# A two-block transformer kernel on one core: first products on the raw stream, 64-row matmuls in pairs, and the class-ordered copy on ScalarE

## The chip, the cores and the metric

The kernel runs on one core of a Trainium2 chip. The metric is the device time of one execution in microseconds (us); lower is better. Several executions of a kernel are timed and the median stands for it.

## What is computed

The reference runs two blocks of two layers each on a stream `x` of 512 tokens by 1024 features. Only the first block is touched. Its layer 0 mixes with gated linear attention (`gla`) and differential attention, its layer 1 with dilated attention over three patterns; each is followed by a feed-forward layer.

```python
def rmsnorm(x, g):
    y = xf * lax.rsqrt(jnp.mean(xf * xf, axis=-1, keepdims=True) + EPS)
    return (y * g.astype(jnp.float32)).astype(x.dtype)
def even_mixer(h, ...):                  # h = rmsnorm(x, norm_mix[0])
    z = h @ w_in                         # aq, ak, av, ag, ar, bq, bk, bv
    log_a = log_sigmoid(ar @ w_a2 + b_a) / GLA_TAU
    oa = rmsnorm(gla(aq, ak, av, log_a), gla_gain) * silu(ag)
    ob = diff_attention(rmsnorm(bq), rmsnorm(bk), bv, lam)   # (softmax(q1 k1^T) - lam softmax(q2 k2^T)) v
    return concat([oa, rmsnorm(ob, diff_gain) * ...]) @ w_out
def odd_mixer(h, ...):                   # q, k normed per head; dilations 1, 4, 16
    ...                                  # dilations 4 and 16 read the tokens by residue class
```

## The kernel before, in words

**Layout.** The stream is kept transposed: eight tiles `x` of 128 features by 512 tokens, in halves of 256 tokens. All large products are float32 made of three fp32r matmuls (`mm3`, line 392): each operand is split into a rounded part and a rest, and hi·hi, hi·lo, lo·hi are added up in one PSUM bank (`gm` by features, `gt` by tokens).

**Weights.** One load of 512 KB (`raw`, four buffers, `wdma`, line 329) holds four 128-row blocks of 256 columns. Two units are cut from it: ScalarE (ACT) copies the rounded part `whi`, VectorE (DVE) subtracts the rest `wlo` (`split`, line 257). A unit serves 12 matmuls of 256 columns in the first passes.

**The norm.** `square` and `norm` (lines 456 and 497) square the stream on ACT into `nsq`, add on DVE, sum over features by a matmul with ones (`nst`), take 1/rms by a chain of 12 small DVE operations (`rsqrt_small`, line 442), spread it by a matmul (`nbc`) to `nrb`, and then make `nt` = x times the norm's weight times `nrb` (DVE), `hh` (ACT) and `hl` (DVE) for each of the eight tiles. In `run` (line 1684) this stands ahead of the first product of the program.

**The first products.** `firsts` (line 707) computes three 256-column weight blocks (k twice, q once) for tokens 0 to 255 and then for tokens 256 to 511: 2 x 144 matmuls of 256 columns, in six banks.

**What sets the order.** The program is written out by a planner in Python: `Clock` (line 98) holds an estimated time of each engine, `tick` (line 771) runs after each tile's matmuls and lets due tasks (`spawn`) and chores (weight splits, rests of intermediate products) issue their next step; `finish` (line 792) steps tasks until given ones are done. Each engine then runs its own instructions in the order written, and waits by semaphores. All instructions carry line 172, that of the wrapper, so this text goes by tile names.

**Even mixer** (line 889). `k_norm` and `q_scale` (lines 944, 989) norm k and prepare q: `qst` (matmul) gives sums of squares of q, a DVE chain on `qv` makes the scale `cc`. `diff_unit` (line 1034) is one head and one block of 128 queries: for each of the two softmaxes a matmul `ds` of 64 rows (float32, two passes) by 128 to 512 columns, then a mask product (`bf_mc`, `bf_ident`), then the softmax. The two softmaxes lie in rows 0 to 63 and 64 to 127 of `q` and `bk`. `gla` (line 1089) makes masked scores `att` and states; `gla_out` (line 1173) is one head: for each of four token tiles one 128-row product `oa<-att,av` and one or two 64-row products `oa<-qd,state`, evacuated to `oraw`, and then `o_norm` (line 974), whose result is split into `mh`, `ml`.

**Odd mixer** (line 1190). The products of the second and third pattern read `ph`, `pl`: `hh`, `hl` with the tokens ordered by class (t mod 4). GpSimd (POOL) makes them by 16 copies of 128x512, issued after the first pattern's q and k. At that time k's norms run on DVE, then the q chains, and PE goes on to the scores `os` and the value products `gt`.

## Time and profile before

| quantity | value |
|---|---|
| median of 3 executions | 3385.5 us (3381.23 to 3389.09) |
| the profiled execution | 3386.47 us |
| its span | 3384.7 us (1.8 us lie around it) |
| busy: PE, weight load, DVE, ACT, POOL | 98%, 86%, 62%, 37%, 1% |
| chain that ended last | PE 89%, DVE 6%, ACT 3%, DMA 1%, issue 1% |

In a timeline row stand the start, the length, the engine, the operation with the tiles it writes and reads, rows\*columns of the array that it uses, the shape that streams, the number of instructions put together, and in brackets the idle time before it with what ended that. A float32 matmul shows as two instructions (two passes). The matmuls overlap at their ends, so a pace is read from starts, not from lengths. In a windows row the clock granted to PE stands as a fraction of its full level.

### The profile page before, as it was taken

The numbers are of one execution on the slowest core, as the hardware profiler recorded it, in microseconds if no ns is written. First come the engines' busy times: TensorE is split into PE (matmuls) and PEld (weight loads), VectorE is DVE, ScalarE is ACT, GpSimd is POOL, SyncE is SP. The second block draws the span as 40 slices with busy tenths as digits, with TensorE's granted clock in tenths as the row PEclk, the third lists the DMA queues.
The fourth block names the chain that finished last, engine by engine and source line by source line (L and its number), as shares of the span: only waits on it lengthen the run. The fifth ranks groups of instructions, "written<-read, shape, count | busy, mean of one in ns | idle before, by whom it ended". The sixth has DMA issues, their size and how long they took to land.

```text
span 3384.7 us, 48370 instructions
## 1 busy us (share of the span) xinstructions
PE 3327.9 (98%) x19172; PEld 2898.5 (86%) x19172; DVE 2113.2 (62%) x4570; ACT 1251.6 (37%) x2526; POOL 28.0 (1%) x29
## 2 busy tenths in 40 slices
PE   7999999989999999999999989999999999999999
PEld 7688888888898888988888987988898889998888
DVE  5757988775669778764455867855663335463333
ACT  5554434334454334322112356422333223443231
POOL 0000000020000000000000000000000000000000
PEclk9999999999999999999999999999999999999999
DMA  3122444412224444443333311344532233222332
GB/s 112 63 63 80 128 141 131 131 63 74 70 88 125 132 136 131 129 146 111 125 119 119 94 42 44 122 153 144 163 100 85 95 100 100 94 89 93 100 99 70
DMA packets 105845, 355.73 MB, mean 105 GB/s; under 512 B 12673, under 2 KB 18962, under 8 KB 105618
## 3 DMA queue, kind: packets, MB, share of 16 engines
q1 hardware_dynamic: 105618, 352.64, 33.2%
q8 instruction: 150, 2.46, 0.3%
q14 instruction: 77, 0.63, 0.1%
HBM read 350.50 MB, written 2.10 MB: 104 GB/s over the span
## 4 chain that ended last, share of the span: by engine, by line
PE 89%; DVE 6%; ACT 3%; issue 1%; DMA 1%; SPq 0%; DVEq 0%; ACTq 0%
PE gm L172 81%; PE gt L172 4%; ACT ap L172 1%; PE ds L172 1%; DVE wlo L172 1%; PE ss L172 1%; DVE nt L172 1%; PE oa L172 1%; DVE amx L172 0%; DVE rs_t L172 0%; PE os L172 0%; ACT L172 0%; DVE ksq L172 0%; DVE x L172 0%; PE opo L172 0%
## 5 line engine op out<-in xcount | busy, mean ns | idle before, releaser
L172 PE MATMUL gm<-hh,whi 128*128 128x512 f32 (+1 forms) x2872 | 1041.0, 362 | 4.9 <-ACT hh L172 4.1
L172 PE MATMUL gm<-hl,whi 128*128 128x512 f32 (+1 forms) x2872 | 1034.5, 360 | 1.2 <-DVE hl L172 1.2
L172 PE MATMUL gm<-hh,wlo 128*128 128x512 f32 (+1 forms) x2872 | 1031.9, 359 | 3.5 <-DVE wlo L172 3.4
L172 DVE TENSOR_TENSOR wlo<-raw,whi 128x512 fp32r<-128x512 f32 (+1 forms) x1028 | 661.7, 681 | 91.9 <-ACT whi L172 91.5
L172 ACT ACTIVATE whi<-raw 128x512 fp32r<-128x512 f32 (+1 forms) x1028 | 581.4, 617 | 291.6 <-PE gm L172 104.8
L172 PEld LDWEIGHTS gm<-hh,wlo 128*128 128x128 f32 x2872 | 543.9, 189 | 87.1 <-DVE wlo L172 4.2
L172 PEld LDWEIGHTS gm<-hh,whi 128*128 128x128 f32 x2872 | 544.7, 190 | 73.5 <-ACT hh L172 4.4
L172 PEld LDWEIGHTS gm<-hl,whi 128*128 128x128 f32 x2872 | 544.7, 190 | 68.4 <-DVE hl L172 1.8
L172 PE MATMUL gm<-mh,whi 128*128 128x512 f32 (+1 forms) x1696 | 577.5, 341 | 0.0
L172 PE MATMUL gm<-ml,whi 128*128 128x512 f32 (+1 forms) x1696 | 573.5, 338 | 1.2 <-DVE ml L172 1.2
L172 PE MATMUL gm<-mh,wlo 128*128 128x512 f32 (+1 forms) x1696 | 572.1, 337 | 0.0
L172 DVE TENSOR_TENSOR ga<-ga,gm 128x512 f32<-128x512 f32 (+1 forms) x110 | 68.1, 633 | 497.5 <-PE gm L172 328.4
L172 PEld LDWEIGHTS gm<-mh,wlo 128*128 128x128 f32 x1696 | 322.2, 190 | 34.8
L172 PEld LDWEIGHTS gm<-ml,whi 128*128 128x128 f32 x1696 | 322.5, 190 | 29.4 <-DVE ml L172 1.6
L172 PEld LDWEIGHTS gm<-mh,whi 128*128 128x128 f32 x1696 | 322.4, 190 | 29.1 <-issue 0.9
L172 ACT ACTIVATE ga<-gm 128x512 f32<-128x512 f32 (+1 forms) x110 | 58.8, 554 | 715.9 <-PE gm L172 715.9
L172 DVE SCALAR_TENSOR_TENSOR macc<-rawm,sc,macc 128x256 f32<-128x256 f32 x504 | 244.0, 484 | 15.4
L172 DVE SCALAR_TENSOR_TENSOR x<-gm,modt,x 128x256 f32<-128x256 f32 (+1 forms) x184 | 106.0, 608 | 226.3 <-PE gm L172 226.2
L172 PEld LDWEIGHTS gm<-hc,whi 128*128 128x128 f32 x736 | 136.0, 190 | 29.0 <-ACT whi L172 1.6
L172 DVE SCALAR_TENSOR_TENSOR cy<-gm,vec,cy 128x511 f32<-128x511 f32 (+1 forms) x176 | 127.8, 747 | 47.9 <-ACT cy L172 44.7
L172 PE MATMUL gm<-hc,whi 128*128 128x256 f32 x736 | 146.2, 282 | 1.4 <-ACT whi L172 1.4
L172 ACT ACTIVATE nsq<-x 128x256 f32<-128x256 f32 x160 | 60.8, 416 | 179.4 <-DVE x L172 175.9
(300 smaller groups left out, 3530.7 us busy)
## 6 DMA issues: line engine op xcount, KB each, us to landing
raw<-in_ffn_w_dram SPq DMA_DIRECT2D x256, 512.0 KB, 4.3
rawm<-in_w_mod_dram SPq DMA_DIRECT2D x144, 512.0 KB, 4.4
raw<-in_ffn_w_up_dram SPq DMA_DIRECT2D x88, 512.0 KB, 3.7
raw<-in_ffn_w_down_dram SPq DMA_DIRECT2D x40, 512.0 KB, 3.7
raw<-in_od_w_in_dram SPq DMA_DIRECT2D x36, 512.0 KB, 3.8
raw<-in_ev_w_in_dram SPq DMA_DIRECT2D x24, 512.0 KB, 3.9
raw<-in_w_in_c_dram SPq DMA_DIRECT2D x16, 512.0 KB, 4.1
raw<-in_w_in_a_dram SPq DMA_DIRECT2D x10, 512.0 KB, 4.5
```

What stands on the lines that cost most here:

```text
L172: return f(*args, **kwargs)
```

## The change

It has three parts.

1. **The start.** The stream is loaded in five transfers instead of sixteen, all loads of the start are put in another order, and the norm's weights (`vec`, 16 columns), the first weight load and a part of the constants are issued on ScalarE's queue. `begin` makes `hh`, `hl` from x times the norm's weight as x lands, with no 1/rms in it; `stats` computes 1/rms (`rs` by token on partitions, `rb` spread over partitions) as a task beside the products. 1/rms is then applied where products are evacuated: `scaled` on DVE for `bk`, `qd`, `kr`, `sg`, `ar`, ACT's `scale` for `bv`, `av`, and three more small DVE operations in each of the four `q_scale` chains. `constants` (POOL) runs after `stats`.
2. **Pairs.** `diff_unit` issues the two 64-row `ds` products back to back in two banks and then the two mask products. `gla_out` handles two heads at once, its 64-row products alternating between rows 0 to 63 and 64 to 127; the four `o_norm` tasks depend on it.
3. **The copy.** The 16 class-ordered copies go from POOL to ACT, as a task `turn` that issues one each 0.9 us of the planner's time.

```diff
-        self.x = []
-        for k in range(NK):
-            t = self.xp.tile([P, S], F32, name=f"x{k}")
-            nc.sync.dma_start(t[:, HALF[0]], a["xT"][k][:, HALF[0]])
-            self.x.append(t)
...
+        nc.scalar.dma_start(self.vec[:, :16], a["vec"][:, :16])
+        load(0, 2, 0)
+        if plan is not None:
+            self.wdma(nc.scalar)
+        load(2, 5, 0)
+        load(5, 8, 0)
+        if plan is not None:
+            self.wdma()
+        load(0, 4, 1)
+        nc.scalar.dma_start(self.cst[:, :256], a["cst"][:, :256])
+        load(4, 8, 1)
         if plan is not None:
             for _ in range(2):
                 self.wdma()
...
+    def begin(self):
...
+        def one(p, k):
+            (hi, lo), x, G = [t[:, HALF[p]] for t in self.hx[k]], self.x[k][:, HALF[p]], self.v("norm_mix", k)
+            nc.scalar.activation(hi, x, AF.Copy, scale=G)
+            nc.vector.scalar_tensor_tensor(lo, x, G, hi.bitcast(F32), op0=OP.mult, op1=OP.subtract)
...
+        for k in range(NK):
+            one(0, k)
+            if k < 4 and k % 2 == 0 and self.plan is not None:
+                self.wsplit()
+                self.flush()
+        self.chore(later())
+        self.stat = self.spawn(self.stats(), front=True, banks=1)
+
+    def stats(self):
...
+                for i in range(2):
+                    nc.scalar.activation(sq[:, i * 256:(i + 1) * 256], self.x[k + i][:, HALF[p]], AF.Square)
+                sums.append(sq)
+                if k:
+                    yield later()
+                    nc.vector.tensor_add(sums[0], sums[0], sq)
...
+    def scaled(self, ps, name, scale=1.0):
+
+        t = self.g(name)
+        self.nc.vector.scalar_tensor_tensor(t, ps, scale, self.rb, op0=OP.mult, op1=OP.mult)
+        return t
...
-        pre = self.firsts([w(8), w(9), w(6)])
+        pre = self.firsts([w(8), w(9), w(6)], [(h, HALF[0], HALF[0], None), (h, HALF[1], HALF[1], self.flush)])
+        self.finish([self.stat])
+        self.constants()
...
+            if rows is not None:
+                by = lambda x: x.rearrange("p (t j) -> p t j", j=nh)
+                rw = rows[:, :, None].to_broadcast([P, 4, nh])
+                nc.vector.tensor_mul(by(v), by(p), rw)
+                nc.vector.tensor_mul(by(v), by(v), rw)
+                p = v
...
-        for j in range(2):
-            s = self.ps("ds", w)
+
+        ss = [self.ps("ds", w) for _ in range(2)]
+        for j, s in enumerate(ss):
             r = slice(j * 64, j * 64 + 64)
             self.mm(s, q[r, n * P:(n + 1) * P], k[r, :w], stop=False)
+        for s in ss:
             self.mm(s[:, n * P:], self.mbf["ident"], self.mbf["mc"], start=False)
...
         for t in range(4):
-            p = self.ps("oa", P)
-            self.mm(p, av[t][:, hd * P:(hd + 1) * P], att[t][:, hd * P:(hd + 1) * P], stop=False)
+            ps = [self.ps("oa", P) for _ in range(2)]
+            for j, p in enumerate(ps):
+                hd = 2 * c + j
+                self.mm(p, av[t][:, hd * P:(hd + 1) * P], att[t][:, hd * P:(hd + 1) * P], stop=False)
             ns = [n for n in (2 * t, 2 * t + 1) if n]
             for n in ns:
-                self.mm(p[:, (n % 2) * 64:(n % 2) * 64 + 64], st[c, n][r, :], qd[c][r, n * 64:n * 64 + 64],
-                        start=False, stop=(n == ns[-1]))
-            nc.scalar.activation(o[:, t * P:(t + 1) * P], p, AF.Copy)
-            yield
-        yield from self.o_norm(o, oa, hd, self.v("gla_gain"), gate=sg)
+                for j, p in enumerate(ps):
+                    r = slice(j * 64, j * 64 + 64)
...
+        def turn():
+            for xs, ys in zip(h, hp):
+                for x, y in zip(xs, ys):
+                    yield self.time() + 0.9
+                    nc.scalar.activation(cls(y), clsps(x), AF.Copy)
...
-                        nc.gpsimd.tensor_copy(cls(y), clsps(x))
+                hp += [(self.h("ph"), self.h("pl")) for _ in range(NK)]
+                turned = self.spawn(turn(), front=True, banks=0)
                 for b in range(2):
                     values(0, b, h)
+                self.finish([turned])
```

**VectorE at the start.** Before the change its rows begin with the norm: the sums of squares, the chain on `rs_y`, one weight rest `wlo`, and then `nt` and `hl` in turn.

```order
L172 TENSOR_TENSOR rs_t<-rs_t,nv 128x2
L172 SCALAR_TENSOR_TENSOR rs_y<-rs_t,rs_y 128x2
L172 TENSOR_TENSOR wlo<-raw,whi 128x512
L172 COPY nrb<-nbc 128x256
L172 SCALAR_TENSOR_TENSOR nt<-x_75,vec,nrb 128x256
L172 SCALAR_TENSOR_TENSOR nt<-x_77,vec,nrb 128x256
L172 SCALAR_TENSOR_TENSOR nt<-x_79,vec,nrb 128x256
L172 SCALAR_TENSOR_TENSOR nt<-x_81,vec,nrb 128x256
L172 TENSOR_TENSOR hl<-nt,hh 128x256
```

With the change the rests `hl` come first, made from x, the weights' table `vec` and `hh`; the third `wlo` (of the second `raw`) stands behind an addition of squares:

```order
L172 SCALAR_TENSOR_TENSOR hl<-x,vec,hh 128x256
L172 TENSOR_TENSOR wlo<-raw,whi 128x512
L172 SCALAR_TENSOR_TENSOR hl<-x,vec,hh 128x256 x2
L172 TENSOR_TENSOR wlo<-raw,whi 128x512
L172 SCALAR_TENSOR_TENSOR hl<-x,vec,hh 128x256 x6
L172 TENSOR_TENSOR nsq<-nsq 128x512
L172 TENSOR_TENSOR wlo<-raw,whi 128x512 x2
L172 SCALAR_TENSOR_TENSOR hl<-x,vec,hh 128x256
L172 TENSOR_TENSOR wlo<-raw,whi 128x512 x2
```

**ScalarE at the same place, with the change.** The addition in DVE's sixth row reads the second pair of squares, and that pair stands behind a `whi` of the third `raw` (the single `whi` between the two pairs):

```order
L172 ACTIVATE hh<-x,vec 128x256 x5
L172 ACTIVATE whi<-raw 128x512 x2
L172 ACTIVATE hh<-x,vec 128x256
L172 ACTIVATE nsq<-x 128x256 x2
L172 ACTIVATE whi<-raw 128x512
L172 ACTIVATE nsq<-x 128x256 x2
L172 ACTIVATE whi<-raw 128x512
```

Before, ACT's squares stood at the top of its program and the products' `hh` behind them; now the squares are spread among the `whi`.

**PE in the differential attention, at the head and query block with 256 keys.** Before, each 64-row product is followed by its mask product:

```order
L172 MATMUL ds<-bk,q 128x256
L172 LDWEIGHTS bf_ident
L172 MATMUL ds<-bf_mc,bf_ident 128x128
L172 MATMUL ds<-bk,q 128x256
L172 LDWEIGHTS bf_ident
L172 MATMUL ds<-bf_mc,bf_ident 128x128
```

With the change the two 64-row products stand together:

```order
L172 MATMUL ds<-bk,q 128x256 x2
L172 LDWEIGHTS bf_ident
L172 MATMUL ds<-bf_mc,bf_ident 128x128
L172 LDWEIGHTS bf_ident
L172 MATMUL ds<-bf_mc,bf_ident 128x128
```

**ScalarE in the odd mixer, with the change.** The copies `ph`, `pl` stand between the softmaxes (`pr`), the evacuations of values (`ov`) and the weights:

```order
L172 ACTIVATE q<-gm,vec 128x512
L172 ACTIVATE ph<-hh 128x512
L172 ACTIVATE pl<-hl 128x512
L172 ACTIVATE ph<-hh 128x512
L172 ACTIVATE pr_7086,sms<-os,nbs,cc 128x128
L172 ACTIVATE pl<-hl 128x512
L172 ACTIVATE ph<-hh 128x512
L172 ACTIVATE pr_7092,sms<-os,nbs,cc 128x128
L172 ACTIVATE whi<-raw 128x512
L172 ACTIVATE pl<-hl 128x512
L172 ACTIVATE pr_7086,sms<-os,nbs,cc 128x256
```

Before, these `pr` followed each other with only `whi` and `ov` between, and POOL's rows ended with the 16 copies, which it no longer has:

```order
L172 MEMSET att 128x512 x4
L172 COPY ph<-hh 128x512
L172 COPY pl<-hl 128x512
L172 COPY ph<-hh 128x512
L172 COPY pl<-hl 128x512
```

## Rows read from the trace of the kernel before

**Rows 1.** First part of the page: busy us (share of span), instructions.
```profile
PE 3327.9 (98%) x19172; PEld 2898.5 (86%) x19172; DVE 2113.2 (62%) x4570; ACT 1251.6 (37%) x2526; POOL 28.0 (1%) x29
```

**Rows 2.** Timeline of PE: start, length, instruction, [idle before <- releaser].
```profile
17.04 0.58 PE L172 MATMUL gm<-hh,whi 128*128 128x256 f32 x1 [4.09 <-ACT hh L172]
...
24.74 0.58 PE L172 MATMUL gm<-hh,wlo 128*128 128x256 f32 x1 [2.89 <-DVE wlo L172]
...
30.03 0.37 PE L172 MATMUL gm<-hl,whi 128*128 128x256 f32 x1
30.24 0.28 PE L172 MATMUL gm<-hh,wlo 128*128 128x256 f32 x1
30.36 0.28 PE L172 MATMUL gm<-hh,whi 128*128 128x256 f32 x1
...
62.31 0.40 PE L172 MATMUL gm<-hh,whi 128*128 128x512 f32 x1
```

**Rows 3.** Timeline of ACT, 0 to 30 us.
```profile
12.13 0.63 ACT L172 ACTIVATE whi<-raw 128x512 fp32r<-128x512 f32 x1 [4.75 <-DMA raw<-in_ev_w_in_dram]
```

**Rows 4.** Windows: engines' busy us, then PEclk, DMA share, GB/s.
```profile
5.00:10.00 5.00, 1.01 (x4) 0.93 (x4) 3.31 (x9) 1.65 (x5) 0.29 (x1) 1.00 0.92 253
...
15.00:20.00 5.00, 2.96 (x12) 2.71 (x12) 3.51 (x11) 4.13 (x12) 0.00 (x0) 1.00 0.97 308
```

**Rows 5.** Groups of 0 to 62.3 us, shapes apart: xcount | busy us, mean ns.
```profile
L172 DVE TENSOR_TENSOR wlo<-raw,whi 128x512 fp32r<-128x512 f32 x19 | 12.1, 688 | 3.5 <-ACT whi L172 3.5
...
L172 DVE SCALAR_TENSOR_TENSOR nt<-x,vec,nrb 128x256 f32<-128x256 f32 x16 | 7.2, 480 | 0.1
...
L172 ACT ACTIVATE nsq<-x 128x256 f32<-128x256 f32 x16 | 6.1, 416 | 3.2 <-DMA x<-in_xT_dram 3.2
...
L172 DVE TENSOR_TENSOR rs_t<-rs_t,nv 128x2 f32<-128x2 f32 x6 | 1.0, 162 | 0.2
```

**Rows 6.** Timeline of PE, 92 to 100 us.
```profile
96.07 0.35 PE L172 MATMUL lam<-lp,cst 128*128 128x2 f32 x2 [1.76 <-DVE lp L172]
```

**Rows 7.** Timeline of PE, 123.6 to 130 us.
```profile
123.65 0.48 PE L172 MATMUL ds<-bk,q 64*128 64x128 f32 x2
124.07 0.23 PE L172 MATMUL ds<-bf_mc,bf_ident 128*128 128x128 bf16 x1
...
126.88 0.70 PE L172 MATMUL ds<-bk,q 64*128 64x256 f32 x2
127.51 0.23 PE L172 MATMUL ds<-bf_mc,bf_ident 128*128 128x128 bf16 x1
```

**Rows 8.** Timeline of PE, 232.5 to 235.5 us.
```profile
233.43 0.67 PE L172 MATMUL kv<-av,el 64*64 64x128 f32 x16
```

**Rows 9.** Timeline of PE, 243 to 252 us.
```profile
246.98 0.66 PE L172 MATMUL oa<-qd,state 64*128 64x64 f32 x4
247.56 0.49 PE L172 MATMUL oa<-att,av 128*128 128x128 f32 x2
```

**Rows 10.** Windows 108 to 295 us.
```profile
112.00:116.00 4.00, 4.00 (x6) 0.92 (x5) 2.54 (x8) 2.31 (x6) 0.00 (x0) 0.52 0.00 0
...
252.00:256.00 4.00, 4.00 (x15) 3.09 (x15) 0.00 (x0) 1.07 (x3) 0.00 (x0) 0.50 0.00 0
```

**Rows 11.** Groups on POOL, 720 to 766 us.
```profile
L172 POOL CAST ph<-hh 128x512 fp32r<-128x512 f32 x8 | 11.6, 1455 | 507.1 <-PE gm L172 507.1
```

**Rows 12.** Groups on DVE, 722 to 745 us.
```profile
L172 DVE TENSOR_TENSOR ksq<-rb 128x512 f32<-128x512 f32 x4 | 5.5, 1374 | 0.0
```

**Rows 13.** PE's waits, 720 to 780 us: us, times, longest.
```profile
PE os L172 <- DVE qv L172: 5.0, 1, 5.0
PE gt L172 <- ACT pr L172: 3.5, 2, 2.1
```

**Rows 14.** Windows 720 to 780 us.
```profile
745.00:750.00 5.00, 5.00 (x24) 4.94 (x25) 4.55 (x15) 0.00 (x0) 2.73 (x3) 0.50 0.00 0
...
760.00:765.00 5.00, 4.80 (x24) 4.63 (x25) 0.10 (x1) 2.34 (x9) 0.00 (x0) 0.59 0.02 3
```

More of the change, by code (lines that the diff above doesn't have):

```diff
@@ L198, in __init__, with load @@
         self.xp = ctx.enter_context(tc.tile_pool(name="stream", bufs=1))
-        self.x = []
-        for k in range(NK):
-            t = self.xp.tile([P, S], F32, name=f"x{k}")
-            nc.sync.dma_start(t[:, HALF[0]], a["xT"][k][:, HALF[0]])
-            self.x.append(t)
+        xs = self.xp.tile([P, NK, S], F32, name="x")
+        self.x = [xs[:, k] for k in range(NK)]
         self.cst = self.cp.tile([P, NCST], F32, name="cst")
-        nc.sync.dma_start(self.cst[:, :256], a["cst"][:, :256])
         self.vec = self.cp.tile([P, NVEC], F32, name="vec")
-        nc.sync.dma_start(self.vec, a["vec"])
+        def load(k0, k1, h):
+            nc.sync.dma_start(xs[:, k0:k1, HALF[h]], a["xT"][k0:k1].rearrange("k p s -> p k s")[:, :, HALF[h]])
+        nc.scalar.dma_start(self.vec[:, :16], a["vec"][:, :16])
[9 more added lines that the diff above has]
+        load(4, 8, 1)
         if plan is not None:
@@ L210, in __init__ @@
                 self.wdma()
-        for k in range(NK):
-            nc.sync.dma_start(self.x[k][:, HALF[1]], a["xT"][k][:, HALF[1]])
-        if plan is not None:
-            for _ in range(2):
-                self.wdma()
+        nc.sync.dma_start(self.vec[:, 16:], a["vec"][:, 16:])
         nc.sync.dma_start(self.cst[:, 256:], a["cst"][:, 256:])
@@ L327, in wsplit, with wdma @@
         self.split_to += 1
-    def wdma(self):
+    def wdma(self, queue=None):
         while self.loaded < len(self.plan) and not self.plan[self.loaded][4]:
@@ L548, in norm, with later @@
                 yield
+    def begin(self):
+        nc = self.nc
+        self.hx = [(self.h("hh"), self.h("hl")) for _ in range(NK)]
+        self.rs, self.rb = self.cp.tile([P, 4], F32, name="rs0"), self.cp.tile([P, S], F32, name="rb0")
+        def one(p, k):
+            (hi, lo), x, G = [t[:, HALF[p]] for t in self.hx[k]], self.x[k][:, HALF[p]], self.v("norm_mix", k)
+            nc.scalar.activation(hi, x, AF.Copy, scale=G)
+            nc.vector.scalar_tensor_tensor(lo, x, G, hi.bitcast(F32), op0=OP.mult, op1=OP.subtract)
+        def later():
+            for k in range(NK):
+                yield
+                one(1, k)
+        for k in range(NK):
+            one(0, k)
[5 more added lines that the diff above has]
+    def stats(self):
+        nc = self.nc
+        later = lambda: self.time() + 0.6
+        for p in range(2):
+            sums = []
+            for k in range(0, NK, 2):
+                yield later()
+                sq = self.g("nsq")
+                for i in range(2):
+                    nc.scalar.activation(sq[:, i * 256:(i + 1) * 256], self.x[k + i][:, HALF[p]], AF.Square)
+                sums.append(sq)
+                if k:
+                    yield later()
+                    nc.vector.tensor_add(sums[0], sums[0], sq)
+            yield later()
+            nc.vector.tensor_add(sums[0][:, :256], sums[0][:, :256], sums[0][:, 256:])
+            yield self.clock.done(sums[0]) if self.plan is not None else None
+            ps = self.ps("nst", 2)
+            for t in range(2):
+                self.mm(ps[:, t:t + 1], sums[0][:, t * P:(t + 1) * P], self.ones[:, 0:1])
+            v, rs = self.s("nv", 2), self.rs[:, 2 * p:2 * p + 2]
+            nc.vector.tensor_scalar(v, ps, 1.0 / D, EPS, op0=OP.mult, op1=OP.add)
+            self.rsqrt_small(v, 2, rs)
+            yield
+            pb = self.ps("nbc", 256)
+            for t in range(2):
+                self.mm(pb[:, t * P:(t + 1) * P], rs[:, t:t + 1].to_broadcast([P, P]), self.ident)
+            nc.vector.tensor_copy(self.rb[:, HALF[p]], pb)
+            yield
     def ready(self, key):
@@ L705, in proj_out, with firsts @@
                 self.update(self.x[2 * b + m], pss[m][0], gate, 2 * b + m)
-    def firsts(self, srcs):
+    def firsts(self, srcs, ps=None):
         res = {}
@@ L712, in did @@
             res[si] = pss
-        self.passes(srcs, NK, self.halves(), did)
+        self.passes(srcs, NK, ps or self.halves(), did)
         self.wb = 8
@@ L933, in even_mixer @@
             for m, ps in enumerate(self.gemm(w(4 + b), NK, H)):
-                t = self.g("sg")
-                nc.scalar.activation(t, ps[0], AF.Silu)
+                t = self.scaled(ps[0], "sg")
+                nc.scalar.activation(t, t, AF.Silu)
                 sg.append(t)
         self.tables(LNEXP)
-        gn = [self.spawn(self.gla_out(gs, hd, sg[hd], oa), [gl]) for hd in range(4)]
+        gn = []
+        for c in range(2):
+            os = [self.g("oraw") for _ in range(2)]
+            go = self.spawn(self.gla_out(gs, c, os), [gl])
+            gn += [self.spawn(self.o_norm(o, oa, 2 * c + j, self.v("gla_gain"), gate=sg[2 * c + j]), [go])
+                   for j, o in enumerate(os)]
         self.finish(dn)
@@ L987, in o_norm, with q_scale @@
         yield
-    def q_scale(self, ps, res, i, gain, mat, nh, dh, perm=None, post=None, front=False):
+    def q_scale(self, ps, res, i, gain, mat, nh, dh, perm=None, post=None, front=False, rows=None):
         nc = self.nc
@@ L1008, in task @@
             self.rsqrt_small(v, 4 * nh, cc)
+            if rows is not None:
+                nc.vector.tensor_mul(by(cc), by(cc), rw)
             res[i] = (q, cc)
@@ L1686, in run @@
         self.hs = {}
[L1687 to L1706 removed]
+        self.begin()
         steps = []
```

48 lines of the change are left out of this document (14 added, 34 removed).

## The prediction

> **What bounds the kernel now.** I read the page's first part, then PE's timeline and its waits, then the windows. The page says that PE is busy 98% of the span [rows 1]. So a change gains only where it fills one of PE's few gaps, lets PE do the same work in less time, or raises the clock that PE is granted. In the timeline of PE the reader is to see three things [rows 2]: the first product starts at 17.04 us; the pace is one matmul of 256 columns per 0.21 us until 30.03 to 30.24 and one per 0.12 us from there on, some 5.3 us after the wait that ends at 24.74; and the first product after `firsts` (the first 512-column one) starts at 62.31. In the odd mixer PE waits 5.0 us for `qv` and 3.5 us for `pr` [rows 13], and behind such gaps the windows show PE at about half the clock [rows 14]. About half the clock stands also in six windows between 108 and 295 us, two from 112 to 119 and four from 248 to 262.5; [rows 10] has one of each.
>
> A difference of 0.2% (6.8 us) is about what measurements of this kernel can tell from none.
>
> **1. The start.** Before, ACT's first `whi` waits for its load until 12.13 [rows 3], and the products wait for the whole norm. After the change a product needs `vec`, x, one `hh` and one `whi`. The first transfers flow from about 2 us on; ahead of `raw` 0 or beside it go 0.26 to 0.65 MB of x. At 253 GB/s [rows 4] that and its own 0.5 MB take 3.0 to 4.6 us, so it lands near 6.0, and with a `whi` of 0.63 [rows 3] PE starts near 6.6, 10.4 us earlier than now. Not all of that stays. `raw` 0 and two matmuls of `raw` 1 are 26 matmuls of 0.21 us: PE is through at 12.1. The third needs the third `wlo`, which on DVE stands behind the addition of squares, and these squares stand on ACT behind a `whi` of `raw` 2 (the order shows it). `raw` 2 is behind 3.6 MB: 2.1 MB at 253 and 1.5 MB at 308 GB/s [rows 4] give 2 + 8.5 + 4.9 = 15.4 us, and between 13.7 and 16.5 with one of the two rates alone. Then come `whi` 0.6, two squares of 0.42, the addition and `wlo`, 0.69 each [rows 3, 5]: 18.3. PE idles 6 us, and the quick pace comes 5.3 us later, as in [rows 2]. Until 23.6 PE does 25 matmuls, and the other 93 of the first pass take 0.12 each, or about 1.5 us more, since DVE also has the second half's eight rests of 0.48 (the `nt` row has their shape) and the chain of 12 small operations [rows 5]: the pass ends at 36.3. The second pass, 144 x 0.12 = 17.3, and the two small products end it at 54.5, against 62.31: **-7.8 us**, between -5 and -10 by the time at which `raw` 2 lands.
>
> That the 1/rms comes late hides: 13 evacuations move to DVE or get a factor there, 13 x 0.69 = 9 us of DVE [rows 5] over the 240 us that follow; in the two windows of [rows 10] it is busy 2.5 and 0 of 4 us. If DVE were full where they fall, they would cost those 9 us; I don't expect it.
>
> **2. q's chain.** Four chains get three more small operations of 0.16 us, 0.20 from start to start: 12 x 0.2 = 2.4 us. The products behind the four chains, with the small `lam` product, wait 1.76 us now for DVE [rows 6]. Part of the delay replaces that wait, since the operation `lam` waits for stands behind the same chains. I take **+0.6**, with 0 and +2.4 as ends.
>
> **3. Pairs of `ds`.** A `ds` product of 128 columns takes 0.42 us up to its mask product, one of 256 columns 0.63 [rows 7]: 0.21 + 0.21 per 128 columns. With the sizes 1 to 4 that is 2.94 us for one head and one softmax, 23.5 us for four heads and two. If the two halves of the array's rows work at the same time, half goes: -11.8. No pair of 64-row products stands in the trace. The nearest row is `kv`: 16 instructions of 64x128 on quadrants of 64x64 in 0.67 us [rows 8]. One such pass alone takes 0.105 us by [rows 7], 16 in turn 1.68. So four run at once, with about 0.2 us left over. I take 0.08 us per pair off for that, 16 x 0.08: **-10.5**. The ends are -13 (the switching between 64 and 128 rows goes from 32 times to 16) and -4.2 (third rival).
>
> **4. Pairs in `gla_out`.** The 128-row products stay. The 64-row ones take 0.58 us for a token tile [rows 9], and some 0.36 in the first tile, which has half as many; if both heads' run together, 2 x (3 x 0.58 + 0.36) = **-4.2**; ends -1 and -6. The half-clock stretch that lies in them stays in my sum.
>
> **5. The four `o_norm`.** They now come in one bunch. Each has five 512-wide DVE operations and a rest, at 0.69 [rows 5] some 4 us a head, 16 in all, with `wlo` and updates between. The last head's `ml` comes later against the shorter PE work. **+1.2**, ends 0 and +4.
>
> **6. The copy.** POOL's copies last 1.46 us each [rows 11], and while they run a DVE operation of 512 columns takes 1.37 us [rows 12] instead of 0.69 [rows 5]. With that gone the k norms and the chains on `qv` end some 11 us earlier, so the 5.0 and 3.5 us of waits go: -8.5. The lower clock behind them costs 5 x (1 - 0.50) + 4.8 x (1 - 0.59) = 4.5 us [rows 14], and goes with them. In exchange ACT gets 16 copies. The trace has no ACT copy that reads every fourth element. The ends are the contiguous copy `whi`, 0.63 [rows 3], and POOL's 1.46 with the same pattern [rows 11]. I take a value near 0.63, since ACT's operations of that size all stand there: 10 us of work. The order has 11 softmaxes, 8 evacuations and 6 `whi` among them, some 14 us of ACT's at 0.4 to 0.63 each; PE has 192 value products of 0.12 and 5 us of scores there, 28 us. It fits, with perhaps one wait of 1 us: **-12.0**; ends -14 and 0 (fourth rival).
>
> **The sum.** -7.8 + 0.6 - 10.5 - 4.2 + 1.2 - 12.0 = -32.7 us. The profiled execution took 3386.5, which gives 3353.8. That execution stands 1.0 above the median of the three, so I say **3353**.
>
> **The rivals.** That the change doesn't do what it says is hardly one: the order shows the pairs, the copies on ACT, and no copies on POOL.
>
> *First: the start gains nothing.* If `raw` 2 lands late (near 20, as a mean rate of 200 GB/s would give), PE stands for 10 us, DVE's work of both halves bunches behind it, and `firsts` ends near 60 to 62. Then 3353 + 7 = 3360. For it: DVE and ACT do the same work as before in less time. Against: loads before ran at 253 to 308 GB/s.
>
> *Second: the clock stays up.* Six windows at half the clock between 108 and 295 cost some 20 us x 0.5 = 10. What ran there were 64-row products one after another [rows 9, 10]; if pairs load the array enough, these 10 come back: 3343. Nothing in the trace shows it.
>
> *Third: pairs overlap by one pass in four.* A float32 product is two passes in the same rows. If a pass can't start before the passes ahead of it in the program, the first product's second pass starts after its first, and only the second product's first pass runs beside it. A `ds` pair then saves one pass, 0.105 us per 128 columns, 4 x 1.05 = 4.2 in all, and `gla_out` some 1.5: 3353 + 6.3 + 2.7 = 3362. Against it stands `kv`: in such an order its 16 passes would need 9 steps of 0.105, 0.95 us, and they took 0.67 [rows 8]. The Trainium skill, "TensorE: Matmul & The Clock Gate", Part 3, states that matmuls start and end strictly in the program's order; by that the sum would come out at 3362. The trace speaks against that reading as far as the two passes go.
>
> *Fourth: ScalarE becomes the bound in the odd mixer.* At 1.46 us a copy, ACT has 23 + 14 = 37 us in 28: PE waits 9 us for `pr` and `ov`, and the clock halves as now. The gain of part 6 goes: 3365.
>
> *Fifth, slower: half the clock for longer.* One mechanism, in the stretch from 107 to 290 us: where PE has small products and short waits its clock is halved, now for some 20 us of it [rows 10]. Shorter PE work makes PE wait more often for softmaxes and norms, and each us at half the clock costs half a us. The change turns slower when such stretches grow by more than 2 x 33 = 66 us; with 90 us more it gives 3353 + 45 = 3398. Against it: the longest such stretch, from 248 to 262.5, ended by itself, with PE never idle in it [rows 10].
>
> **How the numbers follow.** Forecast (3347 to 3359) 0.48; first 0.12; second 0.12; third 0.10; fourth 0.10; fifth 0.04; that new waits eat the gain to within 0.2%, 0.04. Faster by over 0.2% are all but the last two: 0.92; the same 0.04; slower 0.04. For the range I leave out those two and the far parts of the second and of two late rivals together: 3339 to 3371.
>
> **What would show it.** The first `gm` on PE near 6.6 us, a wait for `wlo` of about 6 us that ends near 18, the first 512-column product near 54.5. The second instruction pair of a `ds` group starting within 0.05 us of the first, a pair of 256 columns through in some 0.7 us up to the mask products. No wait over 2 us for `qv` or `pr` in the odd mixer, DVE's 512-wide operations there at 0.69, `ph` and `pl` on ACT under 0.8, and a full clock. The prediction is wrong if PE's work between 107 and 290 us doesn't shrink by 11 to 16 us, or if the odd mixer keeps its gaps with ACT as the one waited for.

## The result, and the profile after

| | before | changed |
|---|---|---|
| median | 3385.92 us (3381.23 to 3389.09, 4 runs) | **3349.65 us** (3348.58 to 3353.55, 4 runs) |
| ratio to before | | 0.9896 [0.9879, 0.9913] |
| the profiled execution's span | 3384.7 us | 3346.8 us |

The changed kernel is faster by 1%, and the time lies 3.4 us under the 3353 that was forecast. A second session of the same kernel gave a median of 3353.9 (3352.79 to 3354.07), so about 4 us of any comparison between sessions mean nothing; the control at the end of the experiments shows where they come from. (A session is a set of kernels timed together.)

The two traces have the same PE instructions, some of them in another order, so the start of one and the same product in both gives a ledger of where the 37.9 us between the two spans came from. (The medians lie 36.3 us apart: the profiled execution of the changed kernel is the fastest of its four.) Before's time of each landmark is in the first column.

| stretch of before | gain in it | forecast |
|---|---|---|
| start to the first 512-column product (62.3) | -10.1 | -7.8 |
| q chains (62 to 106) | +0.1 | +0.6 |
| differential attention (106 to 210) | -6.3 | -10.5 |
| `gla_out` and the norms behind it (232 to 295) | -12.3 | -4.2 + 1.2 |
| the next layer's norm (295 to 312) | +3.8 | 0 |
| odd mixer (695 to 766) | -13.0 | -12.0 |
| all the rest | -0.1 | 0 |

The first part of the page, busy us with shares and instructions, answers to [rows 1]; under it the chain that ended last.

```profile
PE 3295.6 (98%) x19172; PEld 2879.8 (86%) x19172; DVE 2102.9 (63%) x4577; ACT 1260.7 (38%) x2533; POOL 4.9 (0%) x13
...
PE 88%; DVE 7%; ACT 3%; issue 1%; DMA 1%; SPq 0%; DVEq 0%; ACTq 0%
```

PE is 32.3 us less busy with the same 19172 instructions, at the same share. So most of the gain is work that PE does in less time, side by side or at a higher clock, and the smaller part is gaps that went.

**The start.** The timeline of PE, to be held against [rows 2]: start, length, instruction, idle time before it with what ended it.

```profile
7.41 0.58 PE L172 MATMUL gm<-hh,whi 128*128 128x256 f32 x1 [7.41 <-ACT whi L172]
...
12.57 0.31 PE L172 MATMUL gm<-hl,whi 128*128 128x256 f32 x1
...
16.42 0.58 PE L172 MATMUL gm<-hh,wlo 128*128 128x256 f32 x1 [3.19 <-DVE wlo L172]
...
52.24 0.40 PE L172 MATMUL gm<-hh,whi 128*128 128x512 f32 x1
```

The wait for the third `wlo` stands where it was forecast and has the forecast cause, which the timeline of DVE shows: the addition of squares (`nsq`) waits for ScalarE until 15.07, and `wlo` stands behind it.

```profile
15.07 0.69 DVE L172 TENSOR_TENSOR nsq<-nsq 128x512 f32<-128x512 f32 x1 [2.44 <-ACT nsq L172]
15.68 1.29 DVE L172 TENSOR_TENSOR wlo<-raw,whi 128x512 fp32r<-128x512 f32 x2
```

It lasts 3.2 us instead of 6. It ends 1.9 us sooner than forecast, since the transfers ran faster than those of [rows 4], as the last two columns of the windows (DMA share, GB/s) show; and it begins 1.1 us later, since the first product started at 7.41 and not at 6.6. The clock column says 1.00 here only because the trace has no entry of the clock before 12.6 us: a product each 0.21 us is the pace of the half clock, as from 16.4 to 19.4 us, where the entry is 0.50.

```profile
5.00:10.00 5.00, 2.59 (x10) 2.37 (x11) 3.09 (x7) 3.81 (x10) 0.43 (x1) 1.00 1.03 361
10.00:15.00 5.00, 3.23 (x17) 3.03 (x16) 1.97 (x5) 3.93 (x11) 0.00 (x0) 1.00 1.06 389
```

**Differential attention.** The timeline of PE for the first query blocks of a head; [rows 7] has the same products one by one.

```profile
97.27 0.49 PE L172 MATMUL ds<-bk,q 64*128 64x128 f32 x4
97.69 0.29 PE L172 MATMUL ds<-bf_mc,bf_ident 128*128 128x128 bf16 x2
97.91 0.70 PE L172 MATMUL ds<-bk,q 64*128 64x256 f32 x4
98.54 0.28 PE L172 MATMUL ds<-bf_mc,bf_ident 128*128 128x128 bf16 x2
```

Two products of 128 columns take 0.42 us up to the mask products, two of 256 columns 0.63: what one took before. Both passes overlap, not one in four. What it costs stands in PE's waits from 97 to 200 us (total, times, longest). Before there were 0.8 us of waits in this stage; now they are 7.6.

```profile
PE po L172 <- ACT dp L172: 2.6, 2, 1.4
PE gt L172 <- ACT dor L172: 1.9, 1, 1.9
PE ss L172 <- ACT osq L172: 1.8, 1, 1.8
PE dt L172 <- DVE dp L172: 0.8, 1, 0.8
PE gt L172 <- ACT dp L172: 0.5, 1, 0.5
```

What the four longest of them (1.2 to 1.9 us, 6.3 together) hang on shows in the timeline of ACT. Each ends with an ACT operation that stands, in ACT's order, behind one or two loads of ACT's function table (`ACT_TABLE_LOAD`, 1.28 us each) and the operations of a norm or of `log_a` (`lae`). For the wait that ends at 144.78:

```profile
142.53 1.28 ACT L172 ACT_TABLE_LOAD   x1
143.82 0.63 ACT L172 ACTIVATE rb<-rb 128x512 f32<-128x512 f32 x1
144.36 0.37 ACT L172 ACTIVATE dp<-dt 128x256 f32<-128x256 f32 x1
```

DVE is busy up to 95% of a window in this stage (9.5 of 10 us from 130 to 140), but PE doesn't wait there; from 175 to 190, where two of the long waits end, DVE (third pair of numbers) is busy 3.9 of 15 us. No run takes the table loads out, so what they cost is not shown. The seventh column is the granted clock, and where before had half the clock for 6.8 us from 112 us on, it is full; it falls once, at 176 us, behind the wait of 1.9 us.

```profile
100.00:115.00 15.00, 14.07 (x82) 8.17 (x83) 13.04 (x42) 10.04 (x31) 0.00 (x0) 1.00 0.11 35
...
175.00:190.00 15.00, 12.28 (x77) 11.04 (x78) 3.87 (x6) 10.03 (x19) 0.00 (x0) 0.89 0.13 40
...
225.00:240.00 15.00, 15.00 (x114) 12.31 (x113) 4.92 (x9) 8.62 (x25) 0.00 (x0) 1.00 0.24 72
```

**`gla_out`.** A token tile of both heads takes 1.23 us in PE's timeline, of which 0.59 are the 64-row products of both; in [rows 9] those of one head took 0.58. The last window above shows a full clock through it, where before had half of it (second line of [rows 10]).

```profile
232.28 0.66 PE L172 MATMUL oa<-qd,state 64*128 64x64 f32 x8
232.87 0.71 PE L172 MATMUL oa<-att,av 128*128 128x128 f32 x4
233.51 0.66 PE L172 MATMUL oa<-qd,state 64*128 64x64 f32 x8
```

The bunched `o_norm` show up later than forecast. PE's waits from 200 to 300 us have the one for `ml` as before, and two new ones for `hl`, the first products behind the next norm:

```profile
PE gm L172 <- DVE hl L172: 3.4, 2, 1.9
PE gm L172 <- DVE ml L172: 0.8, 1, 0.8
```

**Odd mixer.** Of the 8.5 us of waits in [rows 13] one of 0.5 is left (PE's waits, 700 to 780 us):

```profile
PE gt L172 <- ACT pr L172: 0.5, 1, 0.5
```

The groups on ACT from 720 to 770 us give the price that no row of before had (count | busy us, mean ns):

```profile
L172 ACT ACTIVATE pl<-hl 128x512 fp32r<-128x512 f32 x6 | 7.0, 1159 | 0.0
...
L172 ACT ACTIVATE ph<-hh 128x512 fp32r<-128x512 f32 x5 | 5.8, 1162 | 0.0
```

1.16 us each, not near 0.63. The windows show ACT (fourth pair) busy for 15 us without a gap, with PE nevertheless full from 725 on and the clock up.

```profile
720.00:725.00 5.00, 4.48 (x34) 3.85 (x33) 2.19 (x7) 5.00 (x11) 0.00 (x0) 1.00 0.00 0
725.00:730.00 5.00, 5.00 (x42) 4.71 (x41) 1.78 (x6) 5.00 (x12) 0.00 (x0) 1.00 0.01 3
730.00:735.00 5.00, 5.00 (x43) 4.84 (x42) 2.46 (x7) 5.00 (x9) 0.00 (x0) 1.00 0.45 117
```

### The profile page after: what moved, and what is told of

Same layout as the page of the kernel before. It is cut to its first block, busy times and chain, and to the rows that moved or that the text cites. A ratio compares the mean times of both kernels' runs of the same rounds, so it can differ in the third digit from the quotient of the medians.

```text
span 3346.8 us, 48364 instructions
## 1 busy us (share of the span) xinstructions
PE 3295.6 (98%) x19172; PEld 2879.8 (86%) x19172; DVE 2102.9 (63%) x4577; ACT 1260.7 (38%) x2533; POOL 4.9 (0%) x13
## 4 chain that ended last, share of the span: by engine, by line
PE 88%; DVE 7%; ACT 3%; issue 1%; DMA 1%; SPq 0%; DVEq 0%; ACTq 0%
PE gm L172 80%; PE gt L172 4%; ACT ap L172 1%; DVE wlo L172 1%; DVE nt L172 1%; ACT L172 1%; DVE amx L172 1%; PE ss L172 0%; DVE x L172 0%; DVE rb L172 0%; PE os L172 0%; DVE rs_t L172 0%; DMA raw<-in_ev_w_in_dram 0%; PE opo L172 0%; DVE hl L172 0%
## 5 line engine op out<-in xcount | busy, mean ns | idle before, releaser
L172 DVE SCALAR_TENSOR_TENSOR macc<-rawm,sc,macc 128x256 f32<-128x256 f32 x504 | 244.0, 484 | 15.4
```

The costliest lines, as they stand in the source:

```text
L172: return f(*args, **kwargs)
```

## The experiments

Every kernel is the changed one with one edit, except where the text says otherwise. Times are medians of four runs with the ratio to before. "A" and "B" are the theories that the expectations name.

### One part undone at a time

**`ds` products alone again** (e1_ds_single).

```diff
-        ss = [self.ps("ds", w) for _ in range(2)]
-        for j, s in enumerate(ss):
+        for j in range(2):
+            s = self.ps("ds", w)
             r = slice(j * 64, j * 64 + 64)
             self.mm(s, q[r, n * P:(n + 1) * P], k[r, :w], stop=False)
-        for s in ss:
             self.mm(s[:, n * P:], self.mbf["ident"], self.mbf["mc"], start=False)
```

> The changed kernel with the differential attention's score products one at a time again, everything else kept. Theory A (pairs overlap in full, but the stage's softmaxes on DVE take back half of it): PE's work in the scores grows by about 13 us, the new waits for dp, dor and osq (7.6 us) shrink to 1 to 4, so the time is 4 to 9 us over the changed kernel's 3350: 3354 to 3359. Theory B (the stage is set by DVE alone, the pairs are worth nothing there): 3349 to 3352. If the lower clock seen before in this stage comes from single 64-row products, it is back in the windows and adds some 3 us.

3359.33 us (3357.06 to 3362.05), 0.9921 [0.9907, 0.9936]. The stage from the first `ds` to 192 us of the changed kernel's trace is 10.2 us longer than with pairs: the `ds` and mask products take 13.1 us more and the products behind them 1.2 less, 5.0 us of waits go, and 3.4 us more are lost at the low clock. Of the waits for `dp` 0.3 are left, and the low clock is back in the windows, in the very stretch that has 1.00 with pairs:

```profile
101.00:104.00 3.00, 3.00 (x7) 0.99 (x6) 1.98 (x7) 1.83 (x5) 0.00 (x0) 0.60 0.00 0
104.00:108.00 4.00, 4.00 (x9) 1.17 (x9) 2.17 (x7) 1.22 (x4) 0.00 (x0) 0.50 0.00 0
108.00:112.00 4.00, 4.00 (x11) 1.37 (x10) 3.72 (x13) 1.55 (x4) 0.00 (x0) 0.52 0.42 131
```

So A, at its upper end, and a part of it is clock: PE is busy all the time here and is granted half. The fall comes in a row of single 64-row products (101.6 us); from 107 to 112 us narrow products run in it, on 16 of the array's 128 columns, which run at the full clock behind the pairs:

```profile
106.96 0.77 PE L172 MATMUL gm<-hh,whi 128*16 128x512 f32 x1
```

**`gla_out` by heads again** (e2_oa_single).

```diff
-        for c in range(2):
-            os = [self.g("oraw") for _ in range(2)]
-            go = self.spawn(self.gla_out(gs, c, os), [gl])
...
+        gn = [self.spawn(self.gla_out(gs, hd, sg[hd], oa), [gl]) for hd in range(4)]
...
```

> The changed kernel with the linear attention's output head by head again (its norms spread between the heads as before). Theory A (the pairs keep the clock up): the half-clock stretch of some 13 us is back behind the first heads and costs 6 to 7 us, the lost overlap 4 to 5, while the waits for hl at the next norm (3.4 us) vanish: 3356 to 3359. Theory B (the clock fell before for another reason, such as what ran ahead of it, and stays up): only 4 to 5 less 3.4, 3350 to 3352.

3362.32 us (3361.96 to 3363.5), 0.993 [0.9916, 0.9945], dearer than A said. The stage (232 to 295 us of before) is 14.2 us longer; the same picture in the windows:

```profile
238.00:242.00 4.00, 4.00 (x19) 3.21 (x19) 0.00 (x0) 1.87 (x5) 0.00 (x0) 0.70 0.00 0
242.00:246.00 4.00, 4.00 (x11) 2.53 (x10) 1.29 (x2) 0.88 (x2) 0.00 (x0) 0.50 0.00 0
246.00:250.00 4.00, 4.00 (x12) 3.17 (x13) 0.82 (x2) 2.38 (x6) 0.00 (x0) 0.50 0.41 131
250.00:254.00 4.00, 4.00 (x13) 2.46 (x12) 3.86 (x7) 0.53 (x1) 0.00 (x0) 0.59 0.00 0
```

These four lose 4 x (0.30 + 0.50 + 0.50 + 0.41) = 6.8 us, and the `oa` products themselves take some 5 us more. Both waits for `hl` are gone (3.4 us given back), which ties them to the four norms in a bunch; two others come in their place, for `mh` (0.8) and `ml` (1.4).

**The copies on POOL again** (e3_pool_copy).

```diff
-                turned = self.spawn(turn(), front=True, banks=0)
+                for xs in h:
+                    hp.append((self.h("ph"), self.h("pl")))
+                    for x, y in zip(xs, hp[-1]):
+                        nc.gpsimd.tensor_copy(cls(y), clsps(x))
```

> The changed kernel with the 16 class-ordered copies on POOL again. Theory A (they slow DVE while they run, which delays the q chains, and the clock falls behind the wait): DVE's 512-column operations at 1.3 to 1.6 us beside the copies, waits of 7 to 9 us in the odd mixer, half the clock behind them, 3361 to 3365. Theory B (the waits came from where the planner put the chains, and the copies merely shared the time): under 3355.

3363.27 us (3362.49 to 3363.63), 0.9932 [0.9918, 0.9947], as A said. The odd mixer is 13.2 us longer, DVE's 512-wide operations beside the copies take 1.46 to 1.63 us, and PE's waits are those of [rows 13] again:

```profile
PE os L172 <- DVE qv L172: 5.0, 1, 5.0
PE gt L172 <- ACT pr L172: 3.5, 2, 1.9
```

**The old start with the pairs and the copy** (e4_old_start: `before` with parts 2 and 3 of the change; the diff is against the changed kernel).

```diff
-    def begin(self):
-    def stats(self):
-    def scaled(self, ps, name, scale=1.0):
...
-        pre = self.firsts([w(8), w(9), w(6)], [(h, HALF[0], HALF[0], None), (h, HALF[1], HALF[1], self.flush)])
+        pre = self.firsts([w(8), w(9), w(6)])
...
```

> The kernel before with the pairs and the copy of the change, so without the new start and without 1/rms at evacuation. Theory A (the start is worth its 10 us and its later price on DVE is small): first 512-column product at 62.3, the stages behind it as in the changed kernel, 3358 to 3361. Theory B (the evacuations on DVE cost several us in the differential attention, where DVE is full): the waits for dp shrink by 2 us or more there, 3353 to 3357.

3354.9 us (3353.92 to 3355.89), 0.9907 [0.989, 0.9923]: B's time, but not B's sign. The start is 9.7 us later, yet the kernel only 5.2 slower (and 1.0 slower than the changed kernel's second session). In the two traces, which have equal time at the low clock, the changed kernel's lead is 10.1 us at the first `ds`, 6.7 behind the next norm and 7.3 at the end. Of the 3.5 us given back 3.2 are waits: those for `dp`, `dor` and `osq` come to 5.7 us instead of 7.6 and that for `hl` to 1.2 instead of 3.4, while that for `ml` is 1.6 instead of 0.8. But the waits for `dp` alone are 3.6 us instead of 3.9, not 2 us shorter, so that the evacuations on DVE are the cause is not shown; the planner also puts products of this stage in another order here. This run doesn't separate the loads from the products on the raw stream either.

### How far ScalarE reaches

**Each copy twice** (e7_copy_twice, one run).

```diff
                     yield self.time() + 0.9
-                    nc.scalar.activation(cls(y), clsps(x), AF.Copy)
+                    for _ in range(2):
+                        nc.scalar.activation(cls(y), clsps(x), AF.Copy)
```

> The changed kernel with each class-ordered copy done twice on ACT, 16 more of 1.16 us. Theory A (ACT, busy without a gap from 720 to 735 us, is at its limit there): PE waits for pr, ov or ph some 8 to 16 us, the clock falls behind them, 3358 to 3372. Theory B (the planner and the banks leave slack): under 3354.

3360.85 us; 17.5 us more of ACT's work cost 10.6 us in the odd mixer. PE's waits, 700 to 780 us:

```profile
PE gt L172 <- ACT pr L172: 4.6, 2, 2.6
PE gm L172 <- ACT pl L172: 1.6, 1, 1.6
```

The bound that the fourth rival named is real; it lies somewhere between one copy of 1.16 us and two of 1.13 each.

### Can the new waits be taken out?

**No 1/rms at three evacuations** (e5_no_rms_evac).

```diff
-        gs["q"] = [self.scaled(p[0], "qd", 0.125) for p in self.gemm(w(0), NK, H)]
-        gs["k"] = [self.scaled(p[0], "kr") for p in self.gemm(w(1), NK, H)]
+        gs["q"] = [self.evac(p[0], "qd", scale=0.125) for p in self.gemm(w(0), NK, H)]
+        gs["k"] = [self.evac(p[0], "kr") for p in self.gemm(w(1), NK, H)]
...
-                t = self.scaled(ps[0], "sg")
-                nc.scalar.activation(t, t, AF.Silu)
+                t = self.g("sg")
+                nc.scalar.activation(t, ps[0], AF.Silu)
```

> The changed kernel with the linear attention's q and k and the gate evacuated by ACT alone, so that 1/rms is left out of these three (that part of the computation is missing): 8 evacuations of 0.75 us leave DVE between 100 and 215 us. Theory A (where DVE is full in the differential attention, its late 1/rms costs PE time): the waits for dp, dor and osq (7.6 us in the changed kernel) shrink by 2 to 4, 3346 to 3348. Theory B (those waits hang on the chain of single softmaxes, not on DVE's total): within 1 us of 3350, or slower, since ACT is busy two thirds of that time as well.

3353.65 us (3352.5 to 3354.78), 0.9903 [0.9887, 0.992]: no gain, B. The evacuations go to ACT instead, and the waits only move: `drc` 2.2 us at 154, `dp` 4.2 us at 179 (ended by ACT), `hl` still 1.2. At the wait of 4.2 us neither engine is full (175 to 180 us: DVE busy 3.3, ACT 2.2 of 5): ACT stands idle for 4.1 us until a norm's chain on DVE has ended, and `dp` stands behind that norm's `mh` in ACT's order. So it isn't DVE's total that PE waits for here, as B had it, though the chain is that of a norm and not of softmaxes.

**The second pair's norms later** (e8_second_pair_later).

```diff
-            go = self.spawn(self.gla_out(gs, c, os), [gl])
+            go = self.spawn(self.gla_out(gs, c, os), [gl] + gn)
```

> The changed kernel with the second pair of heads in the linear attention's output begun only when the first pair's norms are done, so that the norms don't come in one bunch. Theory A (the bunch delays the weights' rests and the next norm on DVE, seen as waits of 1.5 and 1.9 us for hl): these waits shrink by 2 to 4 us, 3346 to 3348. Theory B (the bunch only moves: the second pair's norms come later and the final product waits for ml): 3350 to 3354. The clock should stay up in both, since the pairs stand.

3355.57 us (3354.46 to 3355.98), 0.9908 [0.9893, 0.9923]. The bunch is dissolved and the waits for `hl` vanish, but PE now waits 2.1 us for `mh` and 4.3 for `ml`, the end of the last norms. The price changes its place, as theory B had it, and is higher than B's range.

**Sums of squares at half the pace** (e6_adds_later), against the wait of 3.2 us at the start.

```diff
-        later = lambda: self.time() + 0.6
+        later = lambda: self.time() + 1.2
```

> The changed kernel with the planner's delay between the steps of the sums of squares at 1.2 instead of 0.6 us; with that the first addition of squares stands behind the third and fourth wlo on DVE. Theory A (the wait of 3.2 us for wlo at 16.4 us hangs on that addition and so on raw 2): the wait is gone or moves to raw 2's own whi, PE keeps the higher clock that it had just reached, first 512-column product 3 to 5 us earlier than 52.2, 3345 to 3347. Theory B (PE would wait for raw 2 a unit later anyway): under 1 us, 3349 to 3350.

3353.19 us (3349.47 to 3355.27), 0.99 [0.9886, 0.9915]: the gain of A didn't come. One wait became four, 5.9 us together: on DVE `wlo` now stands behind the second half's rests `hl` (six at once) and then behind later additions.

**The second half's rests at a pace of their own.** The rests become a task that issues one in 2.0 us of the planner's time, and the sums get different paces: 2.0 in e9_rests_spread, 1.2 in e10_rests_spread_early, and 2.0 for the first half with 0.6 for the second in e11_sums_two_paces, whose diff stands here.

```diff
             for k in range(NK):
-                yield
+                yield self.time() + 2.0
                 one(1, k)
...
-        self.chore(later())
+        self.rest = self.spawn(later(), front=True, banks=0)
...
-        later = lambda: self.time() + 0.6
+        later = lambda: self.time() + (2.0 if p == 0 else 0.6)
...
-        pre = self.firsts([w(8), w(9), w(6)], [(h, HALF[0], HALF[0], None), (h, HALF[1], HALF[1], self.flush)])
+        pre = self.firsts([w(8), w(9), w(6)], [(h, HALF[0], HALF[0], None), (h, HALF[1], HALF[1], lambda: self.finish([self.rest]))])
```

> The changed kernel with the second half's hh and hl as a task of their own, one tile each 2.0 us of the planner's time instead of all together, and 2.0 instead of 0.6 us between the steps of the sums of squares; so on DVE the third to sixth wlo stand ahead of the second half's rests. Theory A (the first pass waits only for DVE operations that it doesn't need yet): the waits for wlo of 3.2 us and, with the earlier additions moved alone, of 0.8 to 2.0 us four times all go but one for raw 2 or raw 4, PE keeps the higher clock from 13 us on, the first 512-column product starts 4 to 7 us before 52.2, 3343 to 3347. Theory B (the loads set the pace: raw 2 to raw 5 land too late for PE whatever DVE does): 3349 to 3352.

3348.92 us (3346.65 to 3351.71), 0.9891 [0.9874, 0.9907]. The first pass is 6.2 us shorter, with one wait of 0.6 us in it. But the chain behind the sums now ends after the products, and PE waits for it (0 to 55 us):

```profile
PE nbc L172 <- DVE rs L172: 2.5, 1, 2.5
```

> As the kernel with the rests spread, but with 1.2 us between the steps of the sums of squares, so that the first half's chain of 12 small operations stands ahead of the ninth wlo. Theory A: that chain costs up to 2.4 us at the ninth unit, else as with the rests spread: 3344 to 3349. Theory B (the loads set the pace): no difference between the two, 3349 to 3352.

3347.66 us (3346.13 to 3348.81), 0.9889 [0.9874, 0.9904], within A's range: no wait for `rs`, but two for `wlo`, 3.1 us together. e9, e10 and the control below were timed in one session: e9 and e10 lie 5.0 and 6.2 us under the control, and their slowest runs lie under its fastest.

> As the kernel with the rests spread, but the second half's sums of squares at 0.6 us a step again, so that its matmuls nst and nbc stand inside the second pass and not behind it. Theory A (the 6 us gained in the first pass were lost to a wait of 2.5 us for the second half's 1/rms and to the half clock behind it): that wait is gone, the first 512-column product starts at 46 to 48 us instead of 52.2 and the stages behind it as in the changed kernel; 3342 to 3348, at the lower end if the clock stays up. Theory B (the time before the first pass's end is not what the later stages wait for): first product at 46 to 48 but the gain gone by 100 us, 3348 to 3354.

**3344.6 us** (3341.45 to 3346.97), 0.9877 [0.986, 0.9893], as A said, and the fastest kernel here: its slowest run lies under the fastest of the changed kernel's eight, though the intervals of the two ratios overlap. Nor is it luck with the clock: behind the first 13 us its trace has 23.8 us at the low clock, that of the changed kernel 20.4. PE's timeline has one wait of 0.85 us left in the first products, the pace stays quick behind it, and they end 6.0 us sooner:

```profile
12.93 0.39 PE L172 MATMUL gm<-hh,wlo 128*128 128x256 f32 x1 [0.85 <-DVE wlo L172]
13.15 0.28 PE L172 MATMUL gm<-hh,whi 128*128 128x256 f32 x1
...
46.23 0.40 PE L172 MATMUL gm<-hh,whi 128*128 128x512 f32 x1
```

1.0 of the 6.0 us is an earlier first product (6.44), which the edit doesn't touch. 1.2 us go again at 80 us: behind the wait for `qv`, which is as long as before (2.27 us), PE runs at half the pace for 3.4 us.

### The changed kernel once more

> The changed kernel itself once more, as the measure for the two others on this chip: both theories 3348 to 3352.

3353.9 us (3352.79 to 3354.07), 0.9907 [0.9892, 0.9922], above what was expected. The waits are those of the first session to 0.4 us; what differs is the pace behind some of them. PE's timeline of the control behind the wait for `qv`:

```profile
87.35 0.31 PE L172 MATMUL gt<-wlo,hh 128*128 128x256 f32 x1
87.47 0.40 PE L172 MATMUL gt<-whi,hl 128*128 128x256 f32 x1
87.67 0.41 PE L172 MATMUL gt<-whi,hh 128*128 128x256 f32 x1
...
90.87 0.29 PE L172 MATMUL gt<-whi,hh 128*128 128x256 f32 x1
91.00 0.28 PE L172 MATMUL gt<-wlo,hh 128*128 128x256 f32 x1
```

The starts go from 0.12 us apart to 0.21 and back after 3.4 us, behind a wait of 2.28 us. In the first session, behind the same wait of 2.28 us, they stayed at 0.12:

```profile
85.85 0.28 PE L172 MATMUL gt<-whi,hh 128*128 128x256 f32 x1
85.97 0.28 PE L172 MATMUL gt<-wlo,hh 128*128 128x256 f32 x1
86.09 0.28 PE L172 MATMUL gt<-whi,hl 128*128 128x256 f32 x1
```

Three more such places (the start, 188 and 290 us) cost 1.4 to 1.6 us each, together some 5.6 with this one; from 1880 us on the first session's clock falls more often and 1.5 us come back, so the span is 4.2 us longer. So differences of 4 or 5 us between kernels of different sessions decide nothing here, e4, e5 and e6 among them; their readings above rest on the waits. Part of what e9 and e10 gain against the control is these falls as well: at the first 512-column product they lead it by 4.1 and 2.4 us.

## Why the prediction was right

**1. The start: right in place and cause, sized too small.** The step that failed is "15.4" for `raw` 2: it landed at 13.8, with 361 and 389 GB/s in the windows where the prediction took 253 and 308. That the five large transfers of x in place of sixteen are the reason is likely but not shown, since order and queues changed with them. The wait was 3.2 us instead of 6, and the gain -10.1 instead of -7.8, just past the end of its range. What the step called hidden wasn't quite: by the traces of e4 3.5 of the 10.1 us are given back in the stages behind, which wait more; e5 gives no sign that DVE's evacuations are what does it. The first rival (nothing gained) fell.

**2. q's chain.** The longer chain costs 0.1 us here. As forecast, its wait replaces an older one: 2.3 us for `qv` where there were 0.7 for `qv` and 1.8 for `lam` [rows 6].

**3. `ds` pairs: the overlap was larger, the net smaller.** By the starts in the two traces, the low clock taken out, the `ds` and mask products take 13.2 us less, the far end of the range. The third rival, one pass in four, fell: in the trace's single records the four passes of a pair start at 97.268, 97.275, 97.481 and 97.489 us, two and two beside each other. The Trainium skill, "TensorE: Matmul & The Clock Gate", Part 3, says that matmuls start and end strictly in program order; the records don't tell which product a pass belongs to, but a reading in which the second product waits for the first one's second pass doesn't agree with 0.42 us for the pair. What failed is the assumption that the work behind the pairs hides: 6.8 us of new waits (7.6 less 0.8) stand against the gain. The low clock of 112 to 120 us gave back 4 x (0.48 + 0.37) = 3.4 us more, and 0.89 from 175 to 190 took 1.7. These make -8.1. What is left to the measured -6.3 is that the other products of the stage (above all `po`, `ss`, `dt` and the full `gm`) take 1.7 us more in all from start to start, about half of it right at the new waits. e1 prices the pairs from the other side: 13.1 us of work, 10.2 net.

**4. `gla_out`: right on the overlap, wrong on the clock.** The 64-row products take 3.9 us less, where 4.2 were forecast, and the 128-row ones between them 1.0 less. "The half-clock stretch that lies in them stays in my sum" failed: it went, and with it 6.8 us. The second rival, put at 0.12, came true in both its places. It is too narrow in one thing: what ran at half the clock there was not only 64-row products; in the traces narrow products and full 128x512 ones also run in those stretches. e1 and e2 show the cause: with single products the clock falls to 0.50 in the same stretch in which it is 1.00 with pairs, with PE never idle.

**5. The `o_norm` bunch: right to exist, wrong place and size.** It costs 3.8 us at the next norm instead of 1.2 at `ml`. e2 and e8 make it vanish there, and it returns as waits for `mh` and `ml`.

**6. The copy: -13.0 for -12.0, with a price that was off.** The waits give 8.0 us and the clock 5.5, where 8.5 and 4.5 were forecast. A copy takes 1.16 us, nearer to POOL's 1.46 than to 0.63. The reason taken for the lower value (ACT's operations of that size all stand there) failed: none of them read every fourth element, and the pattern is what sets the copies apart from `whi` (0.62), which has the same size and types. The gain came anyway, because PE had enough queued to cover ACT's 15 full us; e7 shows that it doesn't cover twice that work. e3 confirms the rest: DVE's doubled operations, the waits and the clock behind them are all tied to POOL's copies.

**The sum.** -32.7 was forecast, -37.9 came. Too small were the start (2.3), the clock in `gla_out` and its pairs (9.3 with the bunch's 1.2), the copy (1.0) and q's chains (0.5); too large the `ds` pairs (4.2), and the bunch's 3.8 at the next norm was missing. So 13.1 us of misses one way stand against 8.0 the other way, and that the sum came within 5.2 us is in part luck. Of the signs that the prediction named, the full clock in the odd mixer, DVE at 0.69 and the missing waits came; `ph` and `pl` under 0.8 us did not, and PE's work between 107 and 290 us shrank by 16.6 us, a little more than its 11 to 16. The fifth rival, a clock that falls more often, went the other way in this stretch: PE does wait more, but the half-clock stretches shrank.

## What to carry to other kernels

Two matmuls that fill half of the rows each cost as much as one when they stand back to back in different row halves and banks, and a clock that a run of single ones lowers can stay up. What PE saves is worth only what the engines behind it can follow: read on the engine that ends a wait what stands ahead of the awaited operation, and expect part of the gain to come back as short waits there. A wait that was pushed away by rescheduling came back at the next place in e6, e8, e9 and e10, so look for the version in which the engine's work gets its own pace, as in e11, instead of moving one operation.

## What the runs showed of the hardware

- **Half-height products and the clock.** With PE busy without a gap, the clock fell to 0.50, its lower level, in a row of single 64-row float32 products, in e1 (101.6 to 111.8 us) and e2 (239.6 to 253.2 us), and stayed there through other products that followed; with pairs in the same stretches it was 1.00. It is not so everywhere: single ones between other products had 1.00 (before, from 120 us on, [rows 7]).
- **The same wait, two paces.** Behind one and the same wait of 2.28 us the clock stayed up in one session and fell for 3.4 us in another. It cost 1.2 us there; four such places make some 5.6 us in the first 330 us of the two sessions' traces.
- **ScalarE with a stride.** A 128x512 copy that reads every fourth element takes 1.16 us; the contiguous `whi` takes 0.62.
- **A table load on ScalarE.** `ACT_TABLE_LOAD` takes 1.28 us, and it stands in line with the rest of ACT's work: one of them and an `rb` of 0.63 us run on ACT just ahead of the `dp` for which PE waits until 144.78 us.
- **Transfers.** With five loads of the stream between the weights' the windows show 361 to 389 GB/s, with sixteen 253 to 308; order and queues differ too.
